# Recurrence hops of a bidirectional RWKV-7 layer: a block's outputs summed with the two heads' halves exchanged, R's products in turn with the identity products

## The chip, the cores and the metric

The kernel runs on one NeuronCore of a Trainium2 chip. The metric is device time in microseconds (us) of one execution; lower is better. Times of the kernel before: median 1150.76 us of three runs, from 1149.68 to 1152.16. A core has engines that run side by side, each in the order of its own queue: TensorE (PE; its weight loads are shown as PEld), VectorE (DVE), ScalarE (ACT), GpSimd (POOL) and SyncE (SP, which issues transfers). PE takes its operands from SBUF and writes PSUM; a product contracts over the partitions of its operands (up to 128) and puts one row of the result on each PSUM partition.

## The reference, cut to what matters

One layer of a diffusion backbone: a normalisation, one wide projection, a neighbourhood attention branch, a bidirectional RWKV-7 branch, a merge and a gated feed-forward. 512 latent tokens and 128 context tokens go through the same weights. The change lies in the RWKV-7 branch. Per head (8 heads of 64 channels) and per direction a 64 x 64 state `s` runs over the tokens:

```python
def _wkv_step(s, inp):
    r, w, k, v, a, b = inp
    sa = jnp.einsum("bhvk,bhk->bhv", s, a)
    s = s * w[:, :, None, :] + sa[..., None] * b[:, :, None, :] + v[..., None] * k[:, :, None, :]
    return s, jnp.einsum("bhvk,bhk->bhv", s, r)
...
    s_f, y_f = _wkv_scan(s0[:, 0], rh, _heads(decay[:, :, 0]), _heads(k_dir[:, :, 0]), vh,
                         -kk, kk * _heads(iclr[:, :, 0]), False)
    s_b, y_b = _wkv_scan(s0[:, 1], rh, _heads(decay[:, :, 1]), _heads(k_dir[:, :, 1]), vh,
                         -kk, kk * _heads(iclr[:, :, 1]), True)
    y = y_f + y_b
```

`y` is then normalised per head, gets a bonus term and a gate, and goes through an output projection. The final states of the context tokens are an output too.

## The kernel before

**Stages.** The program is written as one stream of instructions per engine. After the input projections and the attention come four recurrence stages (about 296 to 342, 394 to 435, 491 to 533 and 597 to 629 us), one for each channel tile `ct` of 128 channels, that is two heads, `h` = 0 on partitions 0 to 63 and `h` = 1 on partitions 64 to 127 (`hrows[h]`). Between two of them stand the jobs that build the blocks' matrices and invert a triangular one (`n_job`, `g_job`, `v_job`, `t_job`, `inv`). Behind the fourth come the merge, the output projection and the feed-forward, which are almost all large products.

**Blocks and hops.** Tokens are cut into slices `sl` of 64: slices 0 to 7 are the latent tokens, 8 and 9 the context. Each slice has a line `l` per direction `d`. `carry` (L1368 to L1462) takes the state through the slices in eight hops `s` = 0 to 7; hops 0 and 1 also carry slices 8 and 9, so those have four items instead of two. One hop of an item and head does this:

- L1400: `px`, the product of AG with the pair of state and values, ZV (128 partitions contracted, 64 columns). ACT copies it to `x0` (L1403).
- `ysum(back)` (L1380): what the hop before still owed to the outputs, a product of ZV with TG (again 128 partitions), summed into a PSUM tile Y; Y[0] holds the outputs of slices 0 to 7, Y[1] those of 8 and 9.
- L1415, the identity products: the state is copied by an identity matrix into a PSUM tile `pn`, where the state's update will be summed up. Both operands lie on the 64 partitions of head h and the result goes to the same 64: half h of the array's rows into half h of its columns. Slice 8, whose state starts at zero, and slice 7, the last, have none.
- L1421, R's products: the state's part of the outputs, ZV with R_, again from the half h into the half h, summed into Y. Slice 8 has none.
- `yield`, where `weave` may put other work, by a plan of numbers; in nearly all hops it puts none here.
- L1430: Rt with x0, the solution of the block's triangular system; ACT copies it into ZV (L1436). Then a `yield` at which `weave` emits fillers: products of the projection units of later stages (L223, `feat_gen`) and pieces of the next channel tile's preparation (`prep_a` and others; ACT and DVE work with a few products such as L645/L647 and L679).
- L1443: TG with ZV, which completes `pn`; DVE multiplies it by the decay into the next line's ZV (L1455). A `yield` with fillers follows.

At hop 2 ACT copies Y[1] into the output tile `y` (L1406), at the end Y[0] (L1462). `out` reads `y` one stage later at L1472.

**Order.** In these stages the order on PE, ACT, DVE and POOL is the order in which the program is written (`manual_schedule`); an engine waits in its place if an operand isn't there. So a late x0 stops PE at L1430, and a long ACT instruction in front of L1403 makes x0 late. A product with fp32 operands is two instructions of PE with two weight loads; the profile's counts are of instructions (x8 is four products).

Of the kernel before, what the change touches and what calls it, by code (L numbers as in the profile page):

```python
# [108 lines left out]
def V(ap, dims, off=0):  # L109

    return bass.AP(ap.tensor, ap.offset + off, [list(ap.ap[0])] + [list(d) for d in dims])
# [3 lines left out]
def body(ctx: ExitStack, tc: tile.TileContext, xs, xp, cols, consts, w_ada, b_row, w_rw, w_qkv,  # L115
# [3 lines left out]
    pe, act, dve, pool, sp = nc.tensor, nc.scalar, nc.vector, nc.gpsimd, nc.sync  # L119
# [22 lines left out]
    def nm(s):  # L142
        cn[0] += 1
        return f"{s}_{cn[0]}"
# [15 lines left out]
    def idh(h):  # L160
        return K[64 * h:64 * h + 64, KO["ident"] + 64 * h:KO["ident"] + 64 * h + 64]
# [233 lines left out]
    def ada_part(k0, n, c0):  # L395

        for kt in range(0, 8, 4 // n):
            w = wa_load(k0, n, kt)
            yield
            for i in range(4 // n):  # L400
                ada_mm(psa, w[:, i * 256 * n:(i + 1) * 256 * n], kt + i, 64 * n, c0)
# [40 lines left out]
    with s0:  # L442
        with tc.manual_schedule(engines=START):
            g = ada_part(0, 2, 0)
# [21 lines left out]
            g = ada_part(2, 2, 128)  # L466
# [7 lines left out]
            g = ada_part(4, 4, 256)  # L474
# [132 lines left out]
    hrows = (slice(0, 64), slice(64, 128))  # L607
# [232 lines left out]
    with s1:  # L840
# [93 lines left out]
        with ExitStack() as s1b:  # L934
# [128 lines left out]
            with tc.manual_schedule(engines=FIRST):  # L1063
                for k, step in enumerate(PRM["na"].split()):
                    a, p, b, q, n, s_ = (int(x) for x in (step + ".0").split(".")[:6])
# [31 lines left out]
    with ExitStack() as s3:  # L1097
# [7 lines left out]
        R_ = sb.tile([P, 20, 64], F32, name="R_")  # L1105

        TG = sb.tile([P, 20, 2, 2, 64], F32, name="TG")

        ZV = sb.tile([P, 20, 2, 64], F32, name="ZV")
        v = vp0  # L1110

        def out_t():
            return sb.tile([P, 643], F32, tag="out", bufs=2, name=nm("out"))[:, :NT]
# [7 lines left out]
        def wps():  # L1121
            return pp.tile([P, 512], F32, tag="w", bufs=6, name=nm("w"))
# [23 lines left out]
        def line(sl, d):  # L1146

            return sl + (0 if d == 0 else 12 if sl < 8 else 2)
# [219 lines left out]
        def carry(ct, S, last):  # L1368

            Dt = S.Dt  # L1370
            S.y = y = out_t()
            zf = sb.tile([P, 2, 64], F32, tag="zf", bufs=1, name=nm("zf"))
            Y = [wps(), wps()]
            begun, back = [], []

            def ysum(items):

                for (sl, d, l) in items:
                    for h in range(2):
                        pe.matmul(V(Y[sl // 8][hrows[h], :], *ycol(sl, d)), ZV[:, l, h, :], TG[:, l, h, 1, :],  # L1380
                                  start=once(Y[sl // 8], h), stop=sl in (7, 9) and d == 1)

            def once(t, h):
                first = not any(b is t and i == h for b, i in begun)
                begun.append((t, h))
                return first

            def ycol(sl, d):

                n = 8 if sl < 8 else 2  # L1390
                return ([[-1, 64]], 64 * (n - sl % 8) - 1) if d else ([[1, 64]], 64 * (sl % 8))

            for s in range(8):
                items = [(sl, d, line(sl, d)) for sl in ((s, 8 + s) if s < 2 else (s,)) for d in range(2)]
                ng = len(items)

                px = wps()
                for g, (sl, d, l) in enumerate(items):
                    for h in range(2):
                        pe.matmul(px[hrows[h], g * 64:g * 64 + 64], AG[:, l, h, :], ZV[:, l, h, :],  # L1400
                                  start=True, stop=True)
                x0 = sb.tile([P, 4, 64], F32, tag="x0", bufs=2, name=nm("x0"))
                act.copy(x0[:, :ng, :], V(px[:, :], [[64, ng], [1, 64]]))  # L1403
                ysum(back)
                if s == 2:
                    act.copy(y[:, 512:640], Y[1][:, 0:128])  # L1406
                todo = [(g, i) for g, i in enumerate(items) if i[0] != 7]
                if todo:

                    pn = wps()  # L1410
                    for g, (sl, d, l) in todo:
                        for h in range(2):
                            if sl != 8:
                                own = hrows[h]
                                pe.matmul(pn[own, g * 64:g * 64 + 64], idh(h), ZV[own, l, h, :],  # L1415
                                          start=once(pn, h), stop=False)
                for (sl, d, l) in items:
                    for h in range(2):
                        own = hrows[h]
                        if sl != 8:  # L1420
                            pe.matmul(V(Y[sl // 8][own, :], *ycol(sl, d)), ZV[own, l, h, :], R_[own, l, :],  # L1421
                                      start=once(Y[sl // 8], h), stop=False)
                if s == 7 and not PRM["lh"][ct]:
                    last()
                yield
                px = wps()
                for g, (sl, d, l) in enumerate(items):
                    for h in range(2):
                        own = hrows[h]
                        pe.matmul(px[own, g * 64:g * 64 + 64], Rt[own, l, :], x0[own, g, :], start=True, stop=True)  # L1430
                for h in range(2):
                    own = hrows[h]
                    for g, (sl, d, l) in enumerate(items):
                        if g % 2 == 0:
                            dl = items[g + 1][2] - l
                            act.copy(V(ZV[own, l, h, :], [[128 * dl, 2], [1, 64]]),  # L1436
                                     V(px[own, :], [[64, 2], [1, 64]], 64 * g))
                if s == 7 and PRM["lh"][ct]:
                    last()
                yield  # L1440
                for g, (sl, d, l) in todo:
                    for h in range(2):
                        pe.matmul(pn[hrows[h], g * 64:g * 64 + 64], TG[:, l, h, 0, :], ZV[:, l, h, :],  # L1443
                                  start=once(pn, h), stop=g == todo[-1][0])
                for g, (sl, d, l) in todo:
                    if d == 0:
                        dl = line(sl, 1) - l
                        if sl == 9:
                            dve.tensor_tensor(out=zf, in0=V(pn[:, :], [[64, 2], [1, 64]], 64 * g),
                                              in1=V(Dt[:, 0, :], [[dl, 2], [0, 64]], l), op=ALU.mult)  # L1450
                            sp.dma_start(o_st[ct], zf)
                            continue
                        for h in range(2):
                            own = hrows[h]
                            dve.tensor_tensor(out=V(ZV[own, l + 1, h, :], [[128 * dl, 2], [1, 64]]),  # L1455
                                              in0=V(pn[own, :], [[64, 2], [1, 64]], 64 * g),
                                              in1=V(Dt[own, 0, :], [[dl, 2], [0, 64]], l), op=ALU.mult)
                back = items
                if s == 7:
                    ysum(items)  # L1460
                yield
            act.copy(y[:, 0:512], Y[0][:, 0:512])  # L1462

        def out(ct, S):

# [150 lines left out]
        with tc.manual_schedule(engines=FIRST):  # L1616
# [4 lines left out]
            for ct in range(4):  # L1621
# [33 lines left out]
                def last():  # L1655
                    if ct == 3:
                        need("a3")
                    drain(pg)
                    marks.add(f"M{ct + 1}")
                    if ct < 3:  # L1660
                        if PRM["rl"][ct] == 0:
                            need(f"r{ct + 1}", f"v{ct + 1}")
                        for d in range(2):
                            akr(S2, d)
                        if PRM["rl"][ct] == 0:
                            for d in range(2):
                                r_(S2, d, dve)

                hold[0] = True
                weave(carry(ct, S, last), (pg,), PRM["bud"])  # L1670
                hold[0] = False
                og = out(ct, S)
# [343 lines left out]
    with tc.manual_schedule(engines=FIRST):  # L2016
# [5 lines left out]
        for part, fs in enumerate(fts):  # L2022
            old, first, todo = {}, [], [f for f in fs if f >= FA]
# [136 lines left out]
```

## Time and profile before

| | us |
|---|---|
| median of 3 runs | 1150.76 |
| lowest and highest | 1149.68, 1152.16 |
| the profiled execution | 1150.25 |
| its span, first to last instruction | 1148.5 |
| the four recurrence stages together (rows by stretch) | 161.4 |
| PE busy in them | 157.2 |
| mean ns and total of the identity products (L1415), 256 instructions | 235 ns, 13.9 |
| mean ns and total of R's products (L1421), 288 instructions | 225 ns, 14.3 |

The duration of a PE instruction is that of its whole way through the array; instructions overlap, so what a group of them costs is read from the distance of its start to the start of the next group in the timeline, not from the busy time in the table's last two rows. A row of the timeline is: start, length, engine, line, operation, result <- operands, tile of the array or shape, count, and in brackets how long the engine had stood idle before and for whom.

### The profile page before, as it was taken

What the parts mean: (1) busy time and instruction counts of PE and PEld (TensorE: products, weight loads), DVE (VectorE), ACT (ScalarE), POOL (GpSimd) and SP (SyncE); (2) the same over time, 40 slices, a digit from 0 to 9 for tenths busy, and PEclk for the clock granted to TensorE, in tenths of its full rate; (3) what the DMA queues carried; (4) which work ended last, traced back from release to release, by engine and by line L of the source; (5) the groups of instructions that cost most, each with busy time, mean ns of one, the idle gap of its engine ahead of it and who ended that gap; (6) DMA issues with size and microseconds to landing.
All of it is one profiled execution on the core that took longest, in us unless ns stands there. A gap on an engine that the chain in (4) does not pass through costs nothing.

```text
span 1148.5 us, 26859 instructions
## 1 busy us (share of the span) xinstructions
PE 1115.5 (97%) x11160; PEld 989.1 (86%) x11160; DVE 778.9 (68%) x1641; ACT 535.4 (47%) x1052; POOL 195.3 (17%) x262
## 2 busy tenths in 40 slices
PE   6999999999999999999999999999999999999998
PEld 4688878789888988888898788999899989998997
DVE  4565465769558847945786846897478747874775
ACT  4444566655465665556343525654134413441340
POOL 1163244320101202120100521110101010101000
PEclk9999999999999999999999999999999999999999
DMA  9752677654433533343733971223212321232122
GB/s 341 264 119 83 205 277 230 203 150 122 109 75 86 142 91 93 107 108 86 268 108 105 269 213 67 92 93 94 90 56 92 95 90 55 92 96 89 55 92 93
DMA packets 60482, 149.16 MB, mean 130 GB/s; under 512 B 7460, under 2 KB 22436, under 8 KB 60360
## 3 DMA queue, kind: packets, MB, share of 16 engines
q1 hardware_dynamic: 54888, 131.16, 34.8%
q0 software_dynamic: 4032, 14.68, 6.5%
q8 instruction: 88, 1.44, 0.5%
q10 hardware_dynamic: 1440, 1.59, 0.5%
q14 instruction: 34, 0.28, 0.1%
HBM read 118.41 MB, written 14.32 MB: 116 GB/s over the span
## 4 chain that ended last, share of the span: by engine, by line
PE 74%; DVE 10%; issue 8%; ACT 3%; DMA 3%; POOL 1%; SPq 0%; DVEq 0%; ACTq 0%; POOLq 0%
PE acc L311 24%; PE f L1863 21%; PE fl L223 9%; PE mm L223 5%; DVE RL L1321 1%; DVE pr L1317 1%; PE lg L959 1%; PE po L1006 1%; PE pt L988 1%; PE psa L1044 1%; DVE Rt L1353 1%; DMA wa<-in_w_ada_dram 1%; DMA f<-in_w_ada_dram 1%; PE w L1400 1%; PE w L1430 1%
## 5 line engine op out<-in xcount | busy, mean ns | idle before, releaser
L1863 PE MATMUL f<-t,whi 128*128 128x320 f32 x640 | 141.7, 309 | 0.2
L311 PE MATMUL acc<-whi,u 128*128 128x512 f32 (+1 forms) x448 | 136.0, 385 | 0.0
L1863 PE MATMUL f<-b,whi 128*128 128x320 f32 x608 | 135.0, 310 | 0.4 <-DVE b L212 0.4
L223 PE MATMUL fl<-h,whi 128*128 128x320 f32 x672 | 120.8, 320 | 0.0
L1863 PEld LDWEIGHTS f<-t,whi 128*128 128x128 f32 x640 | 106.8, 188 | 0.8 <-issue 0.4
L223 PEld LDWEIGHTS fl<-h,whi 128*128 128x128 f32 x672 | 101.1, 188 | 4.8
L192 ACT CAST whi<-wst 128x1024 fp32r<-128x1024 f32 (+1 forms) x77 | 79.4, 1034 | 54.5 <-PE acc L311 41.8
L1863 PEld LDWEIGHTS f<-b,whi 128*128 128x128 f32 x608 | 101.7, 188 | 1.1 <-issue 0.6
L1863 PE MATMUL f<-t,wlo 128*128 128x320 f32 x320 | 98.9, 309 | 0.0
L311 PEld LDWEIGHTS acc<-whi,u 128*128 128x128 f32 x448 | 83.5, 188 | 16.7
L1863 PE MATMUL f<-b,wlo 128*128 128x320 f32 x304 | 94.0, 309 | 0.0
L1916 ACT CAST whi<-ws 128x1024 fp32r<-128x1024 f32 x40 | 42.1, 1053 | 104.4 <-PE f L1863 45.6
L311 PE MATMUL acc<-wlo,u 128*128 128x512 f32 (+1 forms) x224 | 86.3, 385 | 0.0
L1930 POOL TENSOR_TENSOR ws<-wst 128x512 f32<-128x512 f32 x20 | 29.0, 1449 | 334.9 <-DVE wlo L1919 226.3
L195 DVE TENSOR_TENSOR wlo<-wst,whi 128x1024 fp32r<-128x1024 f32 (+2 forms) x57 | 60.9, 1077 | 30.7 <-ACT whi L192 30.0
L311 PE MATMUL acc<-whi,h 128*128 128x512 f32 x240 | 78.9, 403 | 0.7 <-DVE h L436 0.7
L1731 DVE SCALAR_TENSOR_TENSOR tt<-acc,G 128x512 f32<-128x512 f32 (+1 forms) x51 | 34.7, 680 | 59.3 <-PE acc L311 45.4
L223 PE MATMUL fl<-h,wlo 128*128 128x320 f32 x336 | 63.0, 318 | 0.0
L1916 ACT CAST whi<-wst 128x1024 fp32r<-128x1024 f32 (+1 forms) x48 | 41.4, 870 | 42.3 <-PE acc L311 25.1
L1863 PEld LDWEIGHTS f<-t,wlo 128*128 128x128 f32 x320 | 60.1, 188 | 0.0
L1919 DVE TENSOR_TENSOR wlo<-ws,whi 128x1024 fp32r<-128x1024 f32 x40 | 55.5, 1387 | 5.4 <-ACT whi L1916 5.4
L1455 DVE TENSOR_TENSOR ZV<-w,Dt 64x128 f32<-64x128 f32 x64 | 18.5, 289 | 58.7 <-PE w L1443 57.6
(342 smaller groups left out, 2536.3 us busy)
## 6 DMA issues: line engine op xcount, KB each, us to landing
wst<-in_w_dram SPq DMA_DIRECT2D x66, 512.0 KB
wst<-in_w_rw_dram SPq DMA_DIRECT2D x31, 512.0 KB
wlo<-wst POOLq DMA_DIRECT2D x28, 512.0 KB, 4.9
wa<-in_w_ada_dram SPq DMA_DIRECT2D x24, 512.0 KB
f<-in_w_ada_dram SPq DMA_DIRECT2D x16, 512.0 KB
wst<-in_w_qkv_dram SPq DMA_DIRECT2D x12, 512.0 KB
o<-o_d SPq DMA_DIRECT2D x14, 320.0 KB
x<-in_xs_dram SPq DMA_DIRECT2D x8, 512.0 KB
```

Source lines behind the costliest of these rows:

```text
L192: act.copy(hi[:, :n], st[:, :n])
L195: dve.tensor_tensor(out=lo[:, a:b], in0=st[:, a:b], in1=hi[:, a:b].bitcast(F32), op=ALU.subtract)
L223: pe.matmul(ps[:, :t1 - t0], w[:, a:a + 128], x[:, k0 + kt, t0:t1], start=n == 0, stop=n == 3 * nk - 1)
L311: pe.matmul(pss[i][:, a:b], lhs(x, kt, ts_), w[:, cs_], start=ki == 0 and n == 0, stop=ki == last and n == 2)
L959: pe.matmul(psl[:, hd, o_:o_ + n], qT[ft][rows, qs], x[rows, :], start=True, stop=True)
L988: pe.transpose(pst[:, c * 128:(c + 1) * 128], L[:, c * 128:(c + 1) * 128], ident)
L1455: dve.tensor_tensor(out=V(ZV[own, l + 1, h, :], [[128 * dl, 2], [1, 64]]), in0=V(pn[own, :], [[64, 2], [1, 64]], 64 * g), in1=V(Dt[own, 0, ...
L1731: dve.scalar_tensor_tensor(out=tt, in0=ps[:, a:b], scalar=c, in1=G[:, g, sl], op0=ALU.mult, op1=ALU.mult)
L1863: pe.matmul(ps[:, :H2], w_[:, c_], x_[:, kt, :], start=first and kt + n == 0, stop=last and kt == 3 and n == 2, skip_group_check=more)
L1916: act.copy(r[0][:, :width], src())
L1919: dve.tensor_tensor(out=r[1][:, :width], in0=src(), in1=r[0][:, :width].bitcast(F32), op=ALU.subtract)
L1930: eng_x(PRM["se"][i - 1]).tensor_tensor(out=o_, in0=x, in1=y, op=op)
```

## The change

It touches `carry` alone.

```diff
+            def y_out(i):
+
+                a, n = ((0, 512), (512, 128))[i]
+                for h in range(2):
+                    act.copy(y[hrows[h], a:a + n], Y[i][hrows[1 - h], 0:n])
+
             def ysum(items):
 
                 for (sl, d, l) in items:
                     for h in range(2):
-                        pe.matmul(V(Y[sl // 8][hrows[h], :], *ycol(sl, d)), ZV[:, l, h, :], TG[:, l, h, 1, :],
+                        pe.matmul(V(Y[sl // 8][hrows[1 - h], :], *ycol(sl, d)), ZV[:, l, h, :], TG[:, l, h, 1, :],
                                   start=once(Y[sl // 8], h), stop=sl in (7, 9) and d == 1)
...
                 if s == 2:
-                    act.copy(y[:, 512:640], Y[1][:, 0:128])
+                    y_out(1)
                 todo = [(g, i) for g, i in enumerate(items) if i[0] != 7]
                 if todo:
-
                     pn = wps()
-                    for g, (sl, d, l) in todo:
+                for g, (sl, d, l) in enumerate(items):
+                    if sl == 8:
+                        continue
+                    if sl != 7:
                         for h in range(2):
-                            if sl != 8:
-                                own = hrows[h]
-                                pe.matmul(pn[own, g * 64:g * 64 + 64], idh(h), ZV[own, l, h, :],
-                                          start=once(pn, h), stop=False)
-                for (sl, d, l) in items:
+                            own = hrows[h]
+                            pe.matmul(pn[own, g * 64:g * 64 + 64], idh(h), ZV[own, l, h, :],
+                                      start=once(pn, h), stop=False)
                     for h in range(2):
                         own = hrows[h]
-                        if sl != 8:
-                            pe.matmul(V(Y[sl // 8][own, :], *ycol(sl, d)), ZV[own, l, h, :], R_[own, l, :],
-                                      start=once(Y[sl // 8], h), stop=False)
+                        pe.matmul(V(Y[sl // 8][hrows[1 - h], :], *ycol(sl, d)), ZV[own, l, h, :], R_[own, l, :],
+                                  start=once(Y[sl // 8], h), stop=False)
...
-            act.copy(y[:, 0:512], Y[0][:, 0:512])
+            y_out(0)
```

In Y the outputs of head h now lie on the other head's 64 partitions; R's products go from the array's row half h into its column half 1 - h. `y_out` brings the halves back in place with two copies of 64 partitions each. The number of products is the same.

On PE, hop 1 of the first stage reads as follows before (L1400 `px`, L1380 the y sums into Y[0] = w_3807 and Y[1] = w_3808, L1415 identity into `pn` = w_3918, L1421 R's products, L1430 Rt's; counts are products here):

```order
L1400 MATMUL w_3899<-ZV,AG 64x64 x8
L1380 MATMUL w_3807<-TG,ZV 64x64 x4
L1380 MATMUL w_3808<-TG,ZV 64x64 x4
L1415 MATMUL w_3918<-ZV,K 64x64 x8
L1421 MATMUL w_3807<-R__2901,ZV 64x64 x4
L1421 MATMUL w_3808<-R__2901,ZV 64x64 x4
L1430 MATMUL w_3935<-x_637_3908,Rt 64x64 x8
```

And now, the same hop with the new line numbers (L1422 is the identity, L1426 is R):

```order
L1406 MATMUL w_3899<-ZV,AG 64x64 x8
L1386 MATMUL w_3807<-TG,ZV 64x64 x4
L1386 MATMUL w_3808<-TG,ZV 64x64 x4
L1422 MATMUL w_3918<-ZV,K 64x64 x2
L1426 MATMUL w_3807<-R__2901,ZV 64x64 x2
L1422 MATMUL w_3918<-ZV,K 64x64 x2
L1426 MATMUL w_3807<-R__2901,ZV 64x64 x2
L1422 MATMUL w_3918<-ZV,K 64x64 x2
L1426 MATMUL w_3808<-R__2901,ZV 64x64 x2
L1422 MATMUL w_3918<-ZV,K 64x64 x2
L1426 MATMUL w_3808<-R__2901,ZV 64x64 x2
L1435 MATMUL w_3935<-x_637_3908,Rt 64x64 x8
```

The eight identity products and the eight of R now stand in turn, two (the heads) and two; what precedes and follows them is the same. Hops 0 and 2 to 6 change in the same way with four and four; hop 7 has R's products alone.

On ACT, hop 2 of the first stage before (L1406 is the copy of Y[1], between the copy of x0 and those into ZV):

```order
L674 COPY pre_3858<-r_630_3882 128x320 x2
L1403 COPY x_648_4003<-w_3998 128x128
L1406 COPY out_3805<-w_3808 128x128
L1436 COPY ZV<-w_4023 64x2x64 x2
L702 ACTIVATE P_651_4037<-pre_3885 128x5x64 x2
L705 COPY Dt_3857<-P_651_4037 128x10
```

And now:

```order
L674 COPY pre_3858<-r_630_3882 128x320 x2
L1409 COPY x_648_4003<-w_3998 128x128
L1380 COPY out_3805<-w_3808 64x128 x2
L1441 COPY ZV<-w_4024 64x2x64 x2
L702 ACTIVATE P_651_4038<-pre_3885 128x5x64 x2
L705 COPY Dt_3857<-P_651_4038 128x10
```

One copy of 128 partitions has become two of 64 in the same place. The copy of Y[0] at the end of a stage changes likewise. DVE, POOL and SP keep their order.

## The prediction

> **What bounds the kernel now.** I read the page's busy shares first, then busy time by stretch for the four places where the changed code runs, then what TensorE (PE) waited for between 295 and 630 us.
>
> ```profile
> PE 1115.5 (97%) x11160; PEld 989.1 (86%) x11160; DVE 778.9 (68%) x1641; ACT 535.4 (47%) x1052; POOL 195.3 (17%) x262
> ```
>
> ```profile
> 295.80:342.00 46.20, 44.13 (x594) 38.18 (x594) 20.07 (x40) 28.34 (x72) 6.07 (x10) 0.96 0.31 77
> 393.80:435.00 41.20, 40.05 (x585) 35.03 (x585) 20.28 (x38) 26.42 (x70) 6.64 (x9) 1.00 0.33 89
> 491.00:533.00 42.00, 41.44 (x595) 36.62 (x595) 16.64 (x34) 25.98 (x70) 5.85 (x9) 1.00 0.39 101
> 597.00:629.00 32.00, 31.55 (x527) 26.75 (x527) 20.32 (x50) 11.06 (x35) 0.00 (x0) 1.00 0.39 116
> ```
>
> ```profile
> PE w L1430 <- DVE Rt L1364: 0.8, 1, 0.8
> PE w L1430 <- ACT x L1403: 0.5, 2, 0.3
> ```
>
> In these rows the columns are length, then busy time of PE, PEld, DVE, ACT and POOL with counts, the granted clock, DMA share and GB/s. PE is full in all four recurrence stages (95 to 99%), ACT at most 64%, DVE at most 64%. So PE's time in them is the kernel's time, as long as nothing that PE needs becomes later than PE. The product that consumes the ACT copy x0, L1430, is where that can happen: it is written straight behind the products that change, with no filler in between, and already waited for x0 twice.
>
> **One hop, and what its products cost.** A middle hop of the second stage:
>
> ```profile
> 427.49 0.45 PE L1400 MATMUL w<-ZV,AG 128*64 128x64 f32 x8
> 427.99 0.27 ACT L1403 COPY x<-w 128x128 f32<-128x128 f32 x1 [1.22 <-PE w L1400]
> 428.10 0.45 PE L1415 MATMUL w<-ZV,K 64*64 64x64 f32 x8
> 428.38 0.40 PE L1421 MATMUL w<-R__2901,ZV 64*64 64x64 f32 x8
> 428.62 0.40 PE L1430 MATMUL w<-x,Rt 64*64 64x64 f32 x8
> ```
>
> A written fp32 product is two instructions, so x8 is four products. From the start of the identity group (L1415) to the next group 0.28 us, from R's group (L1421) to the next 0.24: together 0.52. So eight instructions take 0.24 (30 ns each), and the group that follows a change from 128-row to 64-row products takes 0.04 more. Both groups use only two quadrants of the array: half h of the rows into half h of the columns.
>
> The change sends R's products into the other half of the columns and emits them two and two with the identity's, so four products in a row use four different quadrants. The trace has that pattern elsewhere, in the jobs between two recurrence stages:
>
> ```profile
> 445.69 0.57 PE L1259 MATMUL w<-K,f 64*64 64x64 f32 x24
> 446.06 0.27 PE L1211 MATMUL w<-R__2901,f 64*64 64x64 f32 x2
> 447.78 0.22 PE L1248 MATMUL w<-ZV,J 64*64 64x64 f32 x2
> 447.80 0.23 PE L1208 MATMUL w<-AG,f 64*64 64x64 f32 x2
> 447.84 0.23 PE L1248 MATMUL w<-ZV,J 64*64 64x64 f32 x2
> 447.86 0.23 PE L1208 MATMUL w<-AG,f 64*64 64x64 f32 x2
> 447.90 0.30 PE L1211 MATMUL w<-R__2901,f 64*64 64x64 f32 x8
> ```
>
> L1259 starts 24 instructions in 0.37 us, 15 ns each. L1248 and L1208 are the very pattern of the change: same-half products into one PSUM bank in turn with crossed products into another; eight start in 0.12 us, again 15 ns. So I cost the sixteen of a new hop at 16 x 15 ns + 0.04 = 0.28 us, where they now take 0.52: **0.24 us less**. In the hop with slices 1 and 9 everything is double:
>
> ```profile
> 602.59 0.68 PE L1415 MATMUL w<-ZV,K 64*64 64x64 f32 x16
> 603.11 0.63 PE L1421 MATMUL w<-R__2901,ZV 64*64 64x64 f32 x16
> 603.57 0.63 PE L1430 MATMUL w<-x,Rt 64*64 64x64 f32 x16
> ```
>
> 0.98 now, 32 x 15 ns + 0.04 = 0.52 then: **0.46 less**. If the quadrants didn't overlap, both would save nothing; that is the lower bound.
>
> **Where x0 takes it back.** L1430 can't start before x0 is copied. In a free hop x0 starts 0.50 after L1400's first instruction and ends at 0.77; the new L1430 would start at 428.10 + 0.28 = 428.38, and x0 is there at 428.26. Nothing is lost. It is different where ACT is busy with the next channel tile's preparation, or where nothing stands between L1400 and the identity:
>
> ```profile
> 418.85 1.05 ACT L192 CAST whi<-wst 128x1024 fp32r<-128x1024 f32 x1
> 419.79 0.28 ACT L1403 COPY x<-w 128x128 f32<-128x128 f32 x1
> 420.12 0.45 PE L1430 MATMUL w<-x,Rt 64*64 64x64 f32 x8 [0.29 <-ACT x L1403]
> ```
>
> ```profile
> 597.63 0.45 PE L1415 MATMUL w<-ZV,K 64*64 64x64 f32 x8
> 597.75 0.37 ACT L1403 COPY x<-w 128x256 f32<-128x256 f32 x1 [1.52 <-PE w L1400]
> 598.17 0.68 PE L1430 MATMUL w<-x,Rt 64*64 64x64 f32 x16
> ```
>
> In both L1430 starts 0.05 after x0's end (420.07 and 598.12), so it is x0, not PE, that sets it: the gain there is zero and the 0.24 turns into waiting. In the first two stages' first hop it is Rt's copy (the 0.8 us row above), with the same answer. A third kind loses part of two hops:
>
> ```profile
> 410.00 1.49 DVE L696 TENSOR_TENSOR_SCAN pre<-K,pre 128x640 f32<-128x640 f32 x1
> 411.59 0.83 ACT L702 ACTIVATE P<-pre 128x320 f32<-128x320 f32 x2 [0.20 <-DVE pre L696]
> 414.32 0.27 ACT L1403 COPY x<-w 128x128 f32<-128x128 f32 x1
> 414.80 0.40 PE L1430 MATMUL w<-x,Rt 64*64 64x64 f32 x8
> ```
>
> ACT waits for a DVE scan that PE released before the hop ahead, then runs without a gap up to x0, so x0 doesn't come earlier however early PE is. L1430 can move from 414.80 to 414.59 + 0.05: 0.16 for this hop and the one before it together.
>
> **The count.** Of 32 hops, four (slice 7) have no identity products and four (slices 0 and 8) are set by x0 or Rt: nothing. Four are double and free: 4 x 0.46 = 1.84. Of the 20 single ones I find nine free: 9 x 0.24 = 2.16; six in three pairs like the last one, of which one gives 0.16 and the other two between nothing and 0.16, I take half: 0.30 in all; five behind ACT: 0.
>
> **What else moves.** The y sums of the previous hop now take the column halves in the other order than L1400 ahead of them, which a two-quadrant stream may notice at the seam: from nothing to one slot of two instructions (0.06) in each of 28 hops, 1.7 us. The seams between other groups show no such slot; I take a tenth, 0.17. The two y copies become four:
>
> ```profile
> 313.43 0.27 ACT L1406 COPY out<-w 128x128 f32<-128x128 f32 x1 [0.20 <-PE w L1380]
> 314.28 0.55 ACT L1436 COPY ZV<-w 64x128 f32<-64x128 f32 x2 [0.58 <-PE w L1430]
> 628.85 0.59 ACT L1462 COPY out<-w 128x512 f32<-128x512 f32 x1 [0.90 <-PE w L1380]
> 631.19 1.24 PE L1472 MATMUL w<-out,K 128*128 128x320 f32 x4
> ```
>
> Half the partitions take no less time (L1436's two copies of 64x128 take 0.55, the one of 128x128 takes 0.27), so the small copy costs 0.27 more and ends at 313.97, under ACT's 0.58 of idle time even if L1436 comes 0.24 earlier (314.04). The large one costs 0.59 more in the queue, 629.44 becomes 630.03, before its reader at 631.19. Uncovered they would cost 4 x 0.86 = 3.4 us; I take 0. Transfers are not moved.
>
> Sum: 1.84 + 2.16 + 0.30 - 0.17 = **4.1 us less**. PE's waits after these stages (between stages, before the merge) are on engines that PE itself released, so I let all of it through. The profiled execution took 1150.25 us with a span of 1148.5; 1150.25 - 4.1 = 1146.1, and the median of the runs lies 0.5 above that execution: **1146.6**.
>
> **Rivals.** (1) Half of it: ACT and DVE, which now have less of PE to hide behind, hold back more than the three pairs, or the two instructions of a product keep four quadrants from filling. For it: ACT is at 64% and its queue decides 11 of the 20 single hops. Against it: L1248/L1208 run at 15 ns. Half of 4.1 gives 1148.7.
>
> (2) Nothing: the pairs take turns. The products of both row halves go into the same bank. If that made them wait for one another, sixteen would still take 0.52 and the time would be 1150.7. Against it stand L1415, which already writes both row halves into one bank at two per slot, and L1248/L1208, which do it in two banks at once.
> The Trainium skill, in "TensorEngine Tiling (Array Packing)", section "Restrictions and Gotchas", says that different row tiles cannot access the same PSUM bank at the same time. By that rule this rival would be the result; the rows of L1248 and L1208 disagree with it.
>
> (3) Slower. New waits for x0 make PE idle in pieces, and idle PE can lose its clock:
>
> ```profile
> 302.24 1.28 PE L664 MATMUL w<-K,pre 128*128 128x2 f32 x10 [0.68 <-ACT pre L660]
> 304.00:308.00 4.00, 4.00 (x72) 3.69 (x72) 0.00 (x0) 1.66 (x4) 1.99 (x4) 0.61 0.58 164
> ```
>
> Behind 0.68 us of idle time and 1.28 of two-column products the clock fell to 0.61 over 4 us, which costs 0.39 x 4 = 1.6 us. The new waits are about 0.24 in nine hops; if they took the clock three times or more, 4.8 us would outweigh 4.1 and four times would give 1146.6 + 6.4 = 1153. Against it: the 0.29 wait at 420.12 left its stage at clock 1.00.
>
> **How the numbers follow.** Full overlap, as summed: 0.63, between 1144.5 and 1148.2 (no pair held back at one end, a slot of 0.06 at most seams at the other). Half: 0.16. Nothing: 0.11. Slower: 0.10. The time is the likeliest case's, 1146.6. The range from 1144.4 to 1150.0 takes in the first two and leaves out the last two. A measurement here tells about 0.2% (2.3 us) from no change, so faster means below 1148.5: all of the first case and half of the second give 0.70; the other half and the third make 0.19 for the same; 0.11 for slower, with a little for a cause that I don't see.
>
> **What would show it.** In the changed profile identity and R products should alternate and sixteen of them be started in about 0.28 us in every hop; in the nine free hops Rt's product (L1430) should stand 0.24 nearer to the hop's first product (0.89 instead of 1.13 in the hop shown); waits on x0 should grow from 0.5 to some 2.5 us over the four stages; the stages should shrink by 0.8 to 1.6 us each, most in the last, where ACT has least to do. Sixteen still taking 0.5 us would make the theory of quadrants wrong; 0.28 with stages of the old length would mean that the gain is waited away later.

## The result, and the profile after

| | us |
|---|---|
| before, median of 14 runs | 1150.47 (1147.94 to 1154.72) |
| after, median of 14 runs | 1148.33 (1145.05 to 1151.35) |
| ratio | 0.9975, 95% interval 0.9964 to 0.9987 |
| the profiled execution after | 1146.56, span 1144.8 (before: 1150.25, span 1148.5) |

Faster by 2.9 us, with an interval from 1.5 to 4.1; the two profiled executions are 3.7 us apart. A second series of the same kernel, in the experiments below, gave 0.9967 (0.9954 to 0.9981), 3.8 us less.

Busy time by stretch of the kernel after, at the same four places as before (columns: start and end, length, busy time of PE, PEld, DVE, ACT, POOL with counts, granted clock, DMA share, GB/s):

```profile
295.80:342.00 46.20, 43.96 (x615) 37.86 (x614) 22.56 (x44) 29.53 (x75) 6.81 (x10) 1.00 0.34 86
393.80:435.00 41.20, 40.61 (x563) 35.43 (x562) 19.74 (x37) 28.12 (x73) 7.22 (x11) 0.96 0.28 77
491.00:533.00 42.00, 41.10 (x568) 36.10 (x567) 18.23 (x36) 28.68 (x74) 5.29 (x10) 1.00 0.33 91
597.00:629.00 32.00, 31.55 (x499) 26.57 (x498) 22.19 (x51) 13.20 (x40) 0.00 (x0) 1.00 0.35 104
```

PE is busy for 157.2 of these 161.4 us, as before, and still sets the time there. That is no contradiction: a stretch is fixed in time, and when the hops get shorter, later work moves into it. The gain is seen in starts, not in shares. The timeline of the same middle hop of the second stage (L1406 is now `px`, L1409 the copy to x0, L1422 identity, L1426 R, L1435 Rt):

```profile
425.71 0.45 PE L1406 MATMUL w<-ZV,AG 128*64 128x64 f32 x8
426.21 0.27 ACT L1409 COPY x<-w 128x128 f32<-128x128 f32 x1 [1.24 <-PE w L1406]
426.33 0.27 PE L1422 MATMUL w<-ZV,K 64*64 64x64 f32 x2
426.34 0.27 PE L1426 MATMUL w<-R__2901,ZV 64*64 64x64 f32 x2
...
426.55 0.22 PE L1422 MATMUL w<-ZV,K 64*64 64x64 f32 x2
426.57 0.23 PE L1426 MATMUL w<-R__2901,ZV 64*64 64x64 f32 x2
426.61 0.40 PE L1435 MATMUL w<-x,Rt 64*64 64x64 f32 x8
```

R's first pair starts 0.01 behind the identity's first pair, although four identity instructions are written ahead of it. The other twelve instructions follow in fours, 0.06 apart, and Rt's product follows 0.28 after the group began: it stands 0.90 behind the hop's first product, where it stood 1.13. The double hop of the last stage, which took 0.98 for the two groups:

```profile
600.49 0.27 PE L1422 MATMUL w<-ZV,K 64*64 64x64 f32 x2
600.51 0.27 PE L1426 MATMUL w<-R__2901,ZV 64*64 64x64 f32 x2
...
600.96 0.22 PE L1426 MATMUL w<-R__2901,ZV 64*64 64x64 f32 x2
601.01 0.63 PE L1435 MATMUL w<-x,Rt 64*64 64x64 f32 x16
```

0.52. What PE waited for between 295 and 630 us, the row that answers to that of x0 before (total, times, longest):

```profile
PE w L1435 <- ACT x L1409: 1.3, 4, 0.5
```

Going through the hops of both timelines, from a hop's first product to Rt's: the nine free hops lost 0.233 each (2.10 together), the double ones 0.467 (1.87 for four), the three pairs 0.37, 0.11 and 0.18 (0.66), and the others about 0.2 together. That makes 4.8 us in the hops. Two hops of the first stage need a word. The double one ran at half clock in the profile before, so its 0.467 is taken against the kernel in turn without the exchange (below), where it takes 2.06. And in the first hop Rt's first product comes 0.22 earlier, which isn't counted, because the rest of that group still waits for Rt's copy. Laying PE's timelines of before and after over each other shows nearly as much inside the stages: from a stage's first or second hop to its eighth, PE came ahead by 1.03 us in the second stage, 0.85 in the third and 1.53 in the fourth. That is 0.25 less than the 3.66 of the same hops, so a little is lost again behind Rt's products.

### The profile page after: what moved, and what is told of

Its sections match the earlier page's. It is cut to its first block, busy times and chain, and to the rows that moved or that the text cites. A ratio compares the mean times of both kernels' runs of the same rounds, so it can differ in the third digit from the quotient of the medians.

```text
span 1144.8 us, 26869 instructions
## 1 busy us (share of the span) xinstructions
PE 1111.6 (97%) x11160; PEld 983.6 (86%) x11160; DVE 778.3 (68%) x1641; ACT 537.7 (47%) x1060; POOL 195.6 (17%) x262
## 3 DMA queue, kind: packets, MB, share of 16 engines
q8 instruction: 88, 1.44, 0.5%
## 4 chain that ended last, share of the span: by engine, by line
PE 73%; DVE 8%; issue 8%; DMA 6%; ACT 4%; POOL 0%; SPq 0%; ACTq 0%; DVEq 0%; POOLq 0%
PE acc L311 23%; PE f L1868 23%; PE fl L223 9%; PE mm L223 4%; DMA wa<-in_w_ada_dram 3%; DVE RL L1321 1%; DVE pr L1317 1%; PE po L1006 1%; PE psa L1044 1%; PE pt L988 1%; PE lg L959 1%; PE w L1435 1%; DMA win<-in_rpbp_dram 1%; DMA f<-in_w_ada_dram 1%; DMA o<-o_d 1%
## 5 line engine op out<-in xcount | busy, mean ns | idle before, releaser
L1868 PEld LDWEIGHTS f<-b,wlo 128*128 128x128 f32 x304 | 57.1, 188 | 0.1
```

What stands on the lines that cost most here:

```text
L1868: pe.matmul(ps[:, :H2], w_[:, c_], x_[:, kt, :], start=first and kt + n == 0, stop=last and kt == 3 and n == 2, skip_group_check=more)
```

## The experiments

Ten series of runs besides the first one of the change; two of the ten time a kernel once more. Each ratio is to runs of the kernel before made beside that series, so compare ratios, not medians. "Expected" is what stood on record before each ran.

| kernel | ratio to before, 95% interval | median us | span of its profile |
|---|---|---|---|
| the change | 0.9975 (0.9964 to 0.9987) | 1148.33 | 1144.8 |
| the change, second series | 0.9967 (0.9954 to 0.9981) | 1147.05 | 1150.0 |
| in turn, no exchange | 0.9993 (0.9982 to 1.0005) | 1150.41 | 1147.2 |
| exchange, not in turn | 0.9983 (0.9969 to 0.9997) | 1148.61 | 1146.0 |
| change, six x0 copies on DVE | 0.9954 (0.9936 to 0.9971) | 1145.33 | 1142.0 |
| exchange, not in turn, six x0 copies on DVE | 0.9955 (0.9938 to 0.9973) | 1145.45 | 1142.3 |
| before, y copies split | 0.9997 (0.9985 to 1.001) | 1150.42 | 1149.3 |
| change without R's products in hops 0 to 6 | 1.0023 (1.0011 to 1.0035) | 1154.05 | 1151.7 |
| the same, second series | 1.0027 (1.0013 to 1.0041) | 1152.94 | 1150.3 |
| the same, scratch products at the stage's end (R_ and ZV) | 1.0269 (1.0248 to 1.0291) | 1181.85 | 1181.3 |
| the same, scratch products of ZV alone | 0.9997 (0.9984 to 1.0011) | 1150.09 | 1147.4 |

**Which half of the change does it: in turn without the exchange.** The change with R's products, the y sums and `y_out` back in the own half:

```diff
-    pe.matmul(V(Y[sl // 8][hrows[1 - h], :], *ycol(sl, d)), ZV[own, l, h, :], R_[own, l, :],
+    pe.matmul(V(Y[sl // 8][own, :], *ycol(sl, d)), ZV[own, l, h, :], R_[own, l, :],
...
-    act.copy(y[hrows[h], a:a + n], Y[i][hrows[1 - h], 0:n])
+    act.copy(y[hrows[h], a:a + n], Y[i][hrows[h], 0:n])
```

> The change without the exchange: identity and R's products in turn, but R's still from row half h into column half h. Quadrants (my theory): the sixteen instructions of a hop use two quadrants only and take 0.52 us as before (Rt's first product 1.13 us after the hop's first in a free hop); ratio to before 1.000 within 0.001. Rival, the turn-taking itself (two PSUM banks in alternation) is what helps: 0.28 us, Rt's product at 0.90, ratio 0.9975 like the change.

The hop of the second stage in this kernel's timeline:

```profile
426.96 0.33 PE L1422 MATMUL w<-ZV,K 64*64 64x64 f32 x4
427.13 0.28 PE L1426 MATMUL w<-R__2901,ZV 64*64 64x64 f32 x4
427.24 0.28 PE L1422 MATMUL w<-ZV,K 64*64 64x64 f32 x4
427.36 0.28 PE L1426 MATMUL w<-R__2901,ZV 64*64 64x64 f32 x4
427.48 0.34 PE L1435 MATMUL w<-x,Rt 64*64 64x64 f32 x6
```

Identity and R stand in turn, and the sixteen still take 0.52: behind the first, the groups of four start 0.12 apart, 30 ns an instruction. Taking turns within the same two quadrants is worth nothing. 0.9993 can't be told from no change.

**The exchange without the turns.** The change with all identity products ahead of all of R's, as before:

```diff
-                for g, (sl, d, l) in enumerate(items):
-                    if sl == 8:
-                        continue
-                    if sl != 7:
-                        for h in range(2):
+                for g, (sl, d, l) in todo:
+                    for h in range(2):
+                        if sl != 8:
                             own = hrows[h]
                             pe.matmul(pn[own, g * 64:g * 64 + 64], idh(h), ZV[own, l, h, :],
                                       start=once(pn, h), stop=False)
+                for (sl, d, l) in items:
                     for h in range(2):
                         own = hrows[h]
-                        pe.matmul(V(Y[sl // 8][hrows[1 - h], :], *ycol(sl, d)), ZV[own, l, h, :], R_[own, l, :],
-                                  start=once(Y[sl // 8], h), stop=False)
+                        if sl != 8:
+                            pe.matmul(V(Y[sl // 8][hrows[1 - h], :], *ycol(sl, d)), ZV[own, l, h, :], R_[own, l, :],
+                                      start=once(Y[sl // 8], h), stop=False)
```

> The change without the turn-taking: all identity products first, then all of R's, crossed. Quadrants: each group by itself still uses two quadrants, so 0.28 + 0.24; only at a seam between straight and crossed products two pairs may overlap, at most 0.06 us for each of 28 hops at two seams. Rt's product at 1.08 to 1.13 in a free hop instead of 0.90, ratio 0.998 to 1.000, nearer to 1.000 where x0 is late anyway. Rival, crossing the halves alone is what helps: Rt's product at 0.90, ratio 0.9975.

The expectation that followed from the quadrants alone, that products run in the order in which they are written, was wrong. A single hop, then the double hop of the last stage (here L1420 is the identity):

```profile
426.68 0.28 PE L1420 MATMUL w<-ZV,K 64*64 64x64 f32 x2
426.71 0.27 PE L1426 MATMUL w<-R__2901,ZV 64*64 64x64 f32 x2
...
426.97 0.40 PE L1435 MATMUL w<-x,Rt 64*64 64x64 f32 x8
```

```profile
601.61 0.51 PE L1420 MATMUL w<-ZV,K 64*64 64x64 f32 x10
601.90 0.27 PE L1426 MATMUL w<-R__2901,ZV 64*64 64x64 f32 x2
...
602.20 0.27 PE L1435 MATMUL w<-x,Rt 64*64 64x64 f32 x2
```

Eight identity instructions are written ahead of R's first, yet that one starts 0.03 behind the first of the eight. PE lets a later product overtake those that wait for a busy quadrant, as long as its own is free. So PE doesn't keep the order of its queue between products of different quadrants. The reach is limited: in the double hop, with sixteen ahead, R's first starts only when ten of them have started (0.29 later). In both hops six written instructions are passed over. In the double hop Rt's product then follows 0.59 after the group began instead of 0.52, with the last of R's still running beside it, and the next hop starts some 0.12 later than with the turns. So the exchange alone gives the whole of the single hops, and the turns the last 0.12 in each of the four double ones, some 0.5 us in all, which the ratios can't show (0.9983 against 0.9975, overlapping intervals).

The Trainium skill, in "TensorE: Matmul & The Clock Gate", section "Part 3: Packing small matmuls — row/col tiling", has it that only weight loads are pulled ahead and that matmuls start in strict program order. These rows differ from that, and here they decide: in strict order R's first would have started some 0.24 later, and the exchange alone would have gained at most 0.05 a hop.

**The y copies.** Before, with each of the two y copies split in two copies of 64 partitions and nothing else changed.

```diff
-    act.copy(y[:, 512:640], Y[1][:, 0:128])
+    for h in range(2):
+        act.copy(y[hrows[h], 512:640], Y[1][hrows[h], 0:128])
...
-    act.copy(y[:, 0:512], Y[0][:, 0:512])
+    for h in range(2):
+        act.copy(y[hrows[h], 0:512], Y[0][hrows[h], 0:512])
```

> The kernel before with each y copy split into two of 64 partitions, nothing else. Prediction's theory (hidden under ACT's idle time): ratio 1.000. Rival (the copies lie on the path): 4 x 0.86 = 3.4 us more, ratio 1.003.

0.9997. On the path the copies would have cost 3.4 us, ratio 1.003, which lies outside the interval. In the timeline of the kernel after, ACT's rows around the small copy:

```profile
311.42 0.27 ACT L1409 COPY x<-w 128x128 f32<-128x128 f32 x1 [1.54 <-PE w L1406]
311.89 0.53 ACT L1380 COPY out<-w 64x128 f32<-64x128 f32 x2 [0.21 <-PE w L1386]
312.49 0.54 ACT L1441 COPY ZV<-w 64x128 f32<-64x128 f32 x2
```

The copy into ZV still starts 0.45 behind Rt's first product, as it did before; the split copy ends at 312.42, 0.07 ahead of it. It is hidden, but with little to spare.

**What x0 holds back.** The change with the x0 copy of six hops behind a busy ACT given to DVE:

```diff
-    act.copy(x0[:, :ng, :], V(px[:, :], [[64, ng], [1, 64]]))
+    late = (ct, s) in ((0, 3), (0, 5), (1, 3), (1, 4), (2, 4), (2, 5))
+    (dve.tensor_copy if late else act.copy)(x0[:, :ng, :], V(px[:, :], [[64, ng], [1, 64]]))
```

> The change, and in six hops (3 and 5 of the first stage, 3 and 4 of the second, 4 and 5 of the third) x0 is copied by DVE, which is idle there, instead of ACT, whose queue is late. Theory that a late x0 takes the missing gain: Rt's product goes to 0.90 us after the hop's first product in these hops (1.26, 1.28, 1.00, 1.58, 1.18 and 1.46 in the changed kernel), together 2.4 us less; PE's waits for x0 fall from 1.3 us to under 0.3; ratio to before 0.9955, 0.002 under the change's. Rival, the time is given back at the next wait (ZV's copies stand in the same ACT queue): the hops' ends stay where they are, ratio 0.9975 as the change.

One of the six hops, first as it is in the kernel after, then with the copy on DVE:

```profile
516.54 0.45 PE L1406 MATMUL w<-ZV,AG 128*64 128x64 f32 x8
516.74 1.04 ACT L192 CAST whi<-wst 128x1024 fp32r<-128x1024 f32 x1
...
517.67 0.28 ACT L1409 COPY x<-w 128x128 f32<-128x128 f32 x1
518.00 0.39 PE L1435 MATMUL w<-x,Rt 64*64 64x64 f32 x6 [0.39 <-ACT x L1409]
```

```profile
513.28 0.45 PE L1406 MATMUL w<-ZV,AG 128*64 128x64 f32 x8
513.48 1.04 ACT L192 CAST whi<-wst 128x1024 fp32r<-128x1024 f32 x1
...
513.78 0.29 DVE L1410 COPY x<-w 128x128 f32<-128x128 f32 x1 [0.99 <-PE w L1406]
...
514.18 0.34 PE L1436 MATMUL w<-x,Rt 64*64 64x64 f32 x5
```

With ACT's cast of 1.04 us ahead of it x0 ends at 517.95 and Rt's product starts 0.05 behind it, 1.46 after the hop began; with DVE it starts 0.90 after. So in this hop x0 behind the cast took the change's 0.24 and 0.33 more that the kernel before lost there too. The six hops together became 2.1 us shorter, from a hop's first product to Rt's (2.4 were expected: four of them come to 0.90 or 0.94, two only to 1.01), and no wait on x0 is left among the rows of PE's waits. The ratio 0.9954 is 2.4 and 1.5 us below the change's two. By that the kernel is ahead of both; before is well outside its interval, the change's intervals still overlap with it. The six copies on DVE without the exchange were not run, so what they are worth alone is open. The exchange without turns, with the same six copies:

> The exchange alone (identity products all ahead of R's), with the x0 copies of six hops given to DVE. If the turn-taking matters only in the four double hops (0.07 each), this is 0.3 us behind the change with the same six copies (ratio 0.9954): 0.9957. If the turn-taking matters more, between 0.997 and 0.999. In the trace: sixteen instructions in 0.28 in single hops, 0.59 in double ones.

0.9955 as expected; the two can't be told apart.

**Is one series enough.** The change timed once more:

> The change itself, timed once more. The rows of its first profile put 4.8 us of gain in the hops (nine free hops 2.1, four double ones 1.9, pairs and others 0.8). If the short half-clock windows (3.4 us each, about 0.7 of them more per run in the runs so far) and nothing else eat the rest, the ratio is again near 0.9975 (2.9 us less) and the span is about 1 us longer per additional window; if the first series was only unlucky, it is near 0.996 (4.5 us less).

0.9967. The profiled execution of this series was its slowest one, 1151.81 us with a span of 1150.0, 5.2 more than the other profile of the very same program. Laid over each other, the two differ by 1.9 us at the first hop, from the start-up, by 4.4 at the third, and then by 4.44, 4.68, 4.96 and 5.31 in the four stages, the same within 0.03 in all hops of a stage. So the hops repeat exactly, and what differs lies between them. The start-up's 1.9 and the step from 1.9 to 4.4 are for the most part the clock. Busy time by stretch of the first profile of the change, then of the second (the third number from the end is the granted clock):

```profile
304.00:308.00 4.00, 4.00 (x92) 3.67 (x92) 0.15 (x1) 2.47 (x8) 2.11 (x4) 1.00 0.60 128
392.00:400.00 8.00, 7.06 (x74) 6.13 (x73) 3.09 (x9) 4.43 (x10) 0.88 (x1) 0.79 0.46 145
552.00:560.00 8.00, 6.67 (x98) 5.02 (x99) 4.69 (x14) 2.66 (x4) 0.00 (x0) 0.79 1.04 395
```

```profile
40.00:44.00 4.00, 3.96 (x23) 2.02 (x23) 0.42 (x1) 0.00 (x0) 0.61 (x2) 0.64 0.91 340
304.00:312.00 8.00, 7.33 (x114) 6.48 (x110) 1.32 (x5) 4.28 (x10) 2.98 (x5) 0.79 0.54 133
396.00:404.00 8.00, 7.08 (x83) 6.02 (x83) 3.77 (x9) 4.44 (x10) 1.47 (x2) 0.79 0.40 129
558.00:564.00 6.00, 4.69 (x23) 3.62 (x25) 3.34 (x11) 0.55 (x2) 0.00 (x0) 0.72 1.05 410
```

A clock of 0.79 over 8 us or 0.72 over 6 is 1.7 us of clock lost, the same piece at each place (the one at 41 us lies partly behind the stretch shown). The first profile has two; the second has four; before's profile had one at 304 and one in the start-up. They lie at a few thin places, and whether a place gets one differs between executions of one program. Two pieces more are 3.4 of the 5.2 us between the two profiles. They are a part of the spread of some 6 us between runs of one kernel: over the runs of the change, time and mean clock go together with a correlation of -0.77 in the first series and -0.67 in the second, over those of the kernel before only with -0.3 to -0.6. A single pair of profiles can't give the second digit of the gain.

**R's products left out.** To see whether they cost anything once they use the other quadrants: the change without R's products in hops 0 to 6, so that the output lacks the state's part there.

```diff
                             pe.matmul(pn[own, g * 64:g * 64 + 64], idh(h), ZV[own, l, h, :],
                                       start=once(pn, h), stop=False)
+                        continue
                     for h in range(2):
```

> The change with R's products left out in hops 0 to 6 (144 - 16 = 128 products fewer, outputs y lack the state's part there). Quadrants: the identity's eight instructions alone take 0.28 us, as long as all sixteen in turn, so nothing is gained: Rt's product stays at 0.90 in a free hop, ratio 0.9975 as the change. Rival, R's products still cost PE time beside the identity's (at 15 ns each instruction, 0.12 us a hop): Rt's product at 0.78, some 2 us less, ratio 0.9955.

In the hops it is as expected: Rt's product stands at 0.897 with R's products and without them, so eight products over four quadrants cost what four do over two. But the kernel is 2.7 us slower than before and, by the ratios, 5.5 us slower than the change that it was cut from, with 256 instructions of PE fewer. The loss is not in the hops. It was repeated, and then the same number of products put back where they cost little, into scratch banks that nobody reads behind the last hop's y sums:

> The kernel without R's products in hops 0 to 6 once more, to see whether its idle time is a trait of the program or of one execution. Trait: PE idle time put down to nothing in the profile (issue) is again near 10 us, ratio again near 1.002. One execution: 3 to 4 us of it and a ratio of 0.997.

```diff
                 if s == 7:
                     ysum(items)
+                    sc = [wps(), wps()]
+                    for k in range(16):
+                        for h in range(2):
+                            pe.matmul(sc[k % 2][hrows[(h + k) % 2], (k // 2) * 64:(k // 2) * 64 + 64],
+                                      ZV[hrows[h], l, h, :], R_[hrows[h], l, :], start=True, stop=True)
```

> R's products left out of hops 0 to 6 as in the kernel without them, and as many products (32 a stage, into scratch banks that nobody reads) put behind the last hop's y sums. Theory A (the PE idle time that grew to 10.1 us without R's products hangs on how many instructions stand in PE's stream ahead of the bursts of small products): it falls back to 3 to 4 us, and with up to 64 x 15 ns = 1 us a stage for the scratch the time is about 1154 - 7 + 4 = 1151 or less, ratio 0.997 to 1.000. Theory B (it hangs on the hops themselves, which run ahead of other engines): it stays near 10 us and the time is 1154 to 1158, ratio 1.002 to 1.006.

This one says nothing by its time: the scratch products read R_, which by then belonged to the next stage, and PE waited 22.8 us for it, so that 1.0269 fits neither theory. With ZV in the place of R_:

> As the kernel with R's products left out of hops 0 to 6 and 32 scratch products a stage behind the last hop's y sums, but the scratch products read the state ZV alone, so that they wait for nothing that is rewritten for the next stage (the first attempt waited 23 us for R_'s next content). Theory A (idle time hangs on the instructions that stand ahead in PE's stream): issue idle 3 to 4 us as in that first attempt (2.8), and a ratio of 0.997 to 1.000. Theory B (it hangs on the hops having become shorter): near 10 us, ratio 1.003 to 1.006.

PE's waits for nothing that the profile shows (total, times, longest), the three largest rows in the second run without R's products and then with the scratch products:

```profile
PE w L1211 <- issue: 4.2, 3, 2.1
PE w L1189 <- issue: 3.0, 2, 2.4
PE w L1208 <- issue: 1.6, 1, 1.6
```

```profile
PE w L1211 <- issue: 1.4, 2, 0.8
PE w L1189 <- issue: 1.1, 1, 1.1
PE w L1208 <- issue: 1.1, 1, 1.1
```

All such rows together are 10.1 and 10.6 us in the two series without R's products, 2.8 and 4.6 with the scratch (the second a little above the 3 to 4 of theory A), 2.9 after and 4.2 before. The 128 useless products made the kernel 0.3% faster, from 1.0027 to 0.9997 on the same chip; the change's 0.9967 to 0.9975 isn't reached. The waits belong to bursts of small products between the stages, for instance in the second run without R's products:

```profile
350.58 0.28 PE L1248 MATMUL w<-ZV,J 64*64 64x64 f32 x2
352.24 0.27 PE L1248 MATMUL w<-ZV,J 64*64 64x64 f32 x1 [1.38 <-issue]
```

Counted in the matmul instructions that the trace records, from the program's start, this stop stands at number 3503 in both profiles without R's products; in the profile after, the 0.42 us stop in front of L1259 stands at 3503 too, another product. The twelve profiles have 59 such stops, of 0.2 to 2.4 us, and each stands at number 1848 plus a whole multiple of 127.3, within three instructions (5158, 5411 and 5666 with the scratch are 26, 28 and 30 of them; 5284 and 5539 in the second profile without R's products 27 and 29). So the stops hang on the count of instructions ahead, and what stands at those counts decides what they cost.

The profile also has a row for what ends them. Among the DMA queues of its page is one of the kind "instruction" (packets, MB, share of the engines). First the profile after, then the second without R's products:

```profile
q8 instruction: 88, 1.44, 0.5%
q8 instruction: 86, 1.41, 0.5%
```

Its packets have 16384 bytes each, and there are two fewer where 256 matmul instructions and their weight loads are left out. In the traces each of the 59 stops ends 1.2 to 1.6 us after a packet of this queue has landed; for the stop above, which ends at 352.24, that packet ran from 349.99 to 350.93. A moment picked at random stands that close behind one of 88 packets in 1145 us in about 3 of 100 cases. Around a stop the next packet follows after 3.2 to 5.7 us, while 127 instructions of a dense burst take 1.9 at 15 ns each (an estimate from the 15 ns above). So PE's instructions come in blocks, and a dense burst runs through one faster than the next arrives. Without R's products, block ends fall into bursts where none fell with them (4012, 6559 and 7196). Two of those stops, of 2.2 us each in the first profile without R's products, also have a piece of half clock right behind them (at 544 and 588). That the stops go with the blocks is shown by these counts and packets. No run moves the blocks by themselves, without other instructions being added or left out.

## Why the prediction was right, step by step

**The quadrants** held: 0.28 for sixteen instructions in single hops and 0.52 in double ones, as worked out from L1248/L1208. The kernel in turn without the exchange shows that the four quadrants do it. What the prediction put beside it, that the products must be emitted two and two, fell: PE overtakes.

**The count of hops** held for the free ones (2.10 against 2.16), the double ones (1.87 against 1.84) and the four that are set by x0 or Rt: Rt's product stands 0.05 behind x0's end in each hop behind ACT. The three pairs were taken too low, 0.30 (0.32 by its own terms) against 0.66. For the second stage's pair, which the prediction showed, the reading was wrong that ACT runs from the DVE scan to x0 without a gap. The scan starts 1.44 behind the first product of the hop ahead in both kernels. What came earlier is ACT's last work ahead of x0, first before, then after:

```profile
413.48 0.95 ACT L653 ACTIVATE pre<-w,D 128x320 f32<-128x320 f32 x2
411.85 0.92 ACT L653 ACTIVATE pre<-w,D 128x320 f32<-128x320 f32 x2
```

Counted from the first product of the hop ahead that is 4.92 and 4.74. Before, it had waited 0.08 us for PE's L647, less than the views list as a wait, and L647 came 0.23 earlier with the change. So x0 hung on PE after all and came 0.20 earlier.

**The seam** was a term too much: the y sums start 0.28 behind the hop's first instruction in both kernels (L1380 before, L1386 after), so the 0.17 is 0. On the other side, R's last crossed pair runs beside Rt's first, which the prediction put at nothing: 0.05 in slice 7's hops of the second and third stage, 0.03 in the fourth and none in the first, up to where x0 sets the start.

**The waits on x0** grew from 0.5 to 1.3 us, not to 2.5. The wait is counted from the modelled end of PE's last product, so a start put off by 0.24 doesn't show whole. That was a wrong reading of the view, and it touched no term.

**The stages** were to shrink by 0.8 to 1.6 us each, most in the last: 1.03, 0.85 and 1.53 in those that can be compared.

**The sum** of 4.1 is 4.8 in the hops. Of that 2.9 and 3.8 arrived in the two series. Part of the difference is the clock, which the sum had at nothing. The mean granted clock over the runs was 0.9957 and 0.9964 in the two series of the change and 0.9950, 0.9959 and 0.9956 in the three others with the exchange and all of R's products. In the five without the exchange it was 0.9965, 0.9967 and 0.9966 (the kernel before, beside three sets of runs), 0.9972 (in turn, no exchange) and 0.9977 (y copies split). Each of the first five lies below each of the second five. The means over all their runs, 0.9957 and 0.9968, differ by 0.0011 of 1148 us: 1.3 us, with a 95% interval from 0.6 to 1.9. So the third rival came true at a small size, but not by its mechanism. In the two profiles of the change the pieces of half clock between 295 and 630 us stand behind waits that the kernel before has too (for the ACT work of L660 near 302 to 306, for Rt's copy near 394 to 398, for transfers of o_d near 553 to 560), and none behind the two longest waits on x0 (0.51 us at 418, 0.39 at 518). Why kernels with the exchange lose more clock there isn't shown. It isn't the shorter hops alone, since the kernel with ZV's scratch products has them too at 0.9969. Up to 1 us between the hops and the median stays open. The rival's sign, slower on the whole, fell. That 4.1 lies between what the hops gained and what arrived is in part luck: the hops were taken 0.7 too low, and the loss behind them at nothing.

**Rival 1**, half the gain, lies close to the first series' 1148.33, but its reasons don't hold: ACT and DVE held back less than predicted, and nothing was lost to filling. **Rival 2**, that products of two row halves in one bank take turns, fell with the 0.28.

## What to carry to other kernels

Where two groups of small products sit in the same quadrants of the array, look whether one can be sent to the other half of the columns: a pair of copies that can be hidden buys half of the groups' time. Their order matters little while the groups are short, since PE lets a later product into a free quadrant. Before counting such a gain, find for every hop what is late next: six copies moved from ACT to DVE gave 2.1 us in the hops, where the change itself gave 4.8. And when instructions are added or left out, look at PE's waits for "issue" as well: they moved by 7 us here with a change that left the hops as they were.

## What the hardware did that was not expected

- Products overtake: R's first started 0.03 us behind the identity's first with eight instructions written ahead of it, and 0.29 behind it with sixteen ahead. Six were passed over in both.
- Leaving out 256 instructions made the change 5.5 us slower, and as many useless ones brought some 3 us of it back. PE's idle time without a releaser in the profile went from 2.9 to 10 us and to 4.6, and all 59 stops of this kind end 1.2 to 1.6 us after a 16384-byte packet of the instruction queue has landed.
- One program loses 1.7 us of clock in two places or in four, differing by execution, which makes 3.4 of the 5.2 us between its two profiles.
